# A decoder layer on one core: the weight halves of the front and the queries made once, stored in DRAM and loaded for the second group of tokens

## The chip, the core and the metric

The kernel runs on one core of a Trainium2 chip, as one launch. A core has TensorE (PE: matrix products into PSUM), VectorE (DVE), ScalarE (ACT), GpSimd (POOL), SyncE (SP, which here only issues transfers) and 16 DMA engines that move data between DRAM and on-chip memory. The metric is the device time of the launch in microseconds (us). It was 2892.34 us before the change, the median of three runs from 2890.90 to 2897.49.

## The reference, cut to what matters

One layer over 1024 tokens of width 1024, in fp32:

```
h   = x @ w_in                       # 1024 -> 1792: q 512 | k 128 | v 128 | conv a 512 | conv gate 512
att = window_attention(q, k, v)      # window 128, 8 heads, a sink per head, partial rotary
cnv = swish(LN(causal_conv31(a * sigmoid(gate))))
x1  = LN1(alpha * x + concat(att, cnv) @ w_out)
q   = x1 @ peer_query                # 1024 -> 2048: 8 heads x 2 halves x 128
sc  = q . sub_keys                   # 128 scores per head and half
top 16 of each half, then the 16 best of the 16 x 16 sums -> 128 experts per token, softmax gates
r   = alpha * x1 + sum_e gelu(x1 . u[e]) * gate_e * v[e]    # e among 16384 experts
out = LN2(r + sigmoid(r @ ple_gate) * (p @ ple_proj))
```

The three products with w_in, w_out and peer_query are those that the change touches.

## The kernel before

**Products in three parts.** To keep fp32 accuracy, each operand is split in two: a high half, which is a cast to the rounded format fp32r that PE multiplies, and a low half, which is the operand minus that cast. `mm3` (lines 159 to 162) then issues three matmuls per block of 128: high times high, high times low, low times high. `split` (lines 154 to 157) makes the halves: the cast runs on ACT (it is shown as L156), the subtraction on DVE (L152, in the helper `sub`), and the subtraction needs the cast. For a weight page the two are called `wh<-wraw` and `wl<-wraw,wh`.

**Two groups of tokens.** The 1024 tokens are 8 tiles of 128. Group A is tiles 0 to 2 (384 tokens), group B is tiles 3 to 7 (640 tokens). Each goes through the whole front: w_in, attention, convolution, w_out, LN1, queries. After it the experts of group A are fetched row by row with indirect transfers that POOL issues (`row<-in_peer_u_dram`, `row<-in_peer_v_dram`) and used by DVE (L783 for u, L791 for v), while group B goes through all 16384 experts as dense products (`s_early` for u, and a last stage for v), which fill the rest of the time on PE.

**Weight pages.** A page is 1024 x 128, 512 x 256 or 256 x 512 numbers, 512 KB. `w_split` (lines 270 to 278) makes one: it loads it (`wraw`, issued on SP's queue, L273), and splits it into two more pages `wh` and `wl`. All three come from one pool of six buffers (`wpage`, WPAGES = 6), so two weight pages are in work at a time. Per group there are 14 pages of w_in (8 for the convolution, 2 for k and v, 4 for q), 8 of w_out and 16 of peer_query (one per head and half): 38, and 76 in all, since group B loads and splits the same pages again. `by_token` (L281) multiplies pages for q, k, v and w_out; `by_channel` (L295) those of the convolution and the queries.

**Order.** The work is cut into streams (generators) that yield after each step, and the table `ORDER` and a few calls of `weave` say in which order the steps are written: `c0` and `c1` are the w_in pages of the convolution for group A and B, `t0` and `t1` its 31 taps, done on DVE (`s_taps`, L355 and L357, `cv<-hc,cw,cv`), `q0` and `q1` the pages of q, k and v, `a` attention, `l` the convolution's norm, `w` w_out, `n` LN1, `y` the queries of group A, `h` its choice of experts, `u` the dense products. The queries of group B come in the call `weave((s_query(1), 16), (early, UQ), (rows, RQ))`: 16 steps of queries among dense products and gathered rows. The framework's scheduler then orders each engine's instructions with a timeline that it simulates; only POOL keeps the order written. So the order of DVE, ACT, PE and SP can differ from one version of the kernel to another at places that the source doesn't touch.

**Queries.** `s_query` copies a tile's scores out of PSUM on ACT (L570, `S`, two buffers) and finds the 16 largest per half on DVE (`top16`, L526 to L538: `top<-S`, the replacement `rep` at L534, `top<-rep`).

Of the kernel before, what the change touches and what calls it, by code (L numbers as in the profile page):

```python
# [8 lines left out]
F32 = mybir.dt.float32  # L9
# [10 lines left out]
P = 128  # L20
# [3 lines left out]
KD = D // P  # L24
# [47 lines left out]
def n_split(n):  # L72
    k = -(-n // 512)
    while n % k or (n // k) % 2:
        k += 1
    return [(i * (n // k), n // k) for i in range(k)]
# [22 lines left out]
def layer(tc, io):  # L99
    nc = tc.nc  # L100
    out = io["out"]
    w_in, w_out, w_q = io["w_in"][0], io["w_out"][0], io["peer_query"][0]
    x_d, u_d, v_d = io["x"][0], io["peer_u"][0], io["peer_v"][0]
    groups = [GA, GB]

# [2 lines left out]
    DR = stack.enter_context(tc.tile_pool(name="dram", bufs=1, space=DRAM))  # L108
# [25 lines left out]
    def pt():  # L134
        return PP.tile([P, 512], F32, name="pt")
# [8 lines left out]
    def ph():  # L144
        return PP.tile([P, 512], F32, name="ph", bufs=4)

    def pv():
        return PP.tile([P, 512], F32, name="pv")

    def sub(eng, o, a, b):  # L150

        return eng.tensor_tensor(o, a, b, op=OP.subtract)  # L152

    def split(hi, lo, src, eng):

        nc.scalar.copy(hi, src)  # L156
        return sub(eng, lo, src, hi.bitcast(F32))

    def mm3(ps, lh, ll, rh, rl, first, last):
        nc.tensor.matmul(ps, lh, rh, start=first, stop=False)  # L160
        nc.tensor.matmul(ps, lh, rl, start=False, stop=False)  # L161
        nc.tensor.matmul(ps, ll, rh, start=False, stop=last)  # L162
# [22 lines left out]
    def page(shape, dt, name):  # L185
        return PG.tile(shape, dt, name=name, tag="page", bufs=PAGES)

    def wpage(shape, dt, name):
        return WP.tile(shape, dt, name=name, tag="wpage", bufs=WPAGES)

    def kv(shape, name):
        return WP.tile(shape, F32, name=name, tag="kv", bufs=3)
# [75 lines left out]
                nc.tensor.transpose(ps[:, k * P:(k + 1) * P], src[:, (h + k) * P:(h + k + 1) * P], ident)  # L268
            split(dst[0][:, h:h + 4, sl], dst[1][:, h:h + 4, sl], ps.rearrange("p (k t) -> p k t", k=4), nc.vector)

    def w_split(src, k, n):
        raw = wpage([P, k, n], F32, "wraw")
        nc.sync.dma_start(raw, src.rearrange("(k p) n -> p k n", p=P))  # L273
        hi = wpage([P, k, n], F32R, "wh")
        lo = wpage([P, k, n], F32R, "wl")
        split(hi, lo, raw, nc.vector)
        return hi, lo

    def by_token(gi, src, c0, cn, sink_fn):

        g, (aH, aL) = groups[gi], act[gi]  # L281
        pss = [(ph() if j < 4 else pv())[:, :cn] for j in range(len(g))]
        kn = D // cn
        for kq in range(KD // kn):
            wh, wl = w_split(src[P * kn * kq:P * kn * (kq + 1), c0:c0 + cn], kn, cn)
            for j in range(len(g)):
                sl = slice(j * P, (j + 1) * P)
                for k in range(kn):
                    kk = kn * kq + k
                    mm3(pss[j], aH[:, kk, sl], aL[:, kk, sl], wh[:, k, :], wl[:, k, :], kk == 0, kk == KD - 1)  # L290
                if kk == KD - 1:
                    sink_fn(g[j], pss[j])
            yield

    def by_channel(gi, src, c0, sink_fn):  # L295

        aH, aL = act[gi]
        wh, wl = w_split(src[:, c0:c0 + P], KD, P)
        for (t0, tn) in n_split(len(groups[gi]) * P):
            ps = ph()[:, :tn]  # L300
            for k in range(KD):
                mm3(ps, wh[:, k, :], wl[:, k, :], aH[:, k, t0:t0 + tn], aL[:, k, t0:t0 + tn], k == 0, k == KD - 1)
            sink_fn(ps, t0, tn)
# [8 lines left out]
    def s_qkv(gi):  # L312
        def put_q(i, ps):
            nc.scalar.copy(work[i][:, :512], ps)

        def put_kv(i, ps):
            nc.scalar.copy(
                work[i][:, 512:768].rearrange("p (g u d) -> p g u d", g=2, u=2),
                ps[:, :P].rearrange("p (g d) -> p g d", g=2)[:, :, None, :].to_broadcast([P, 2, 2, 64]))
            vt[i] = work[i][:, 768:896] if i != NA - 1 else W_.tile([P, P], F32, name="vlast")  # L320
            nc.scalar.copy(vt[i], ps[:, P:])

        yield from by_token(gi, w_in, 512, 256, put_kv)
        yield from by_token(gi, w_in, 0, 512, put_q)

    cv, cin = {}, {}

    def s_conv(gi):

        n = len(groups[gi]) * P  # L330
        for bl in range(4):
            sg = W_.tile([P, n], F32, name="sg", bufs=3)
            by_channel(
                gi, w_in, 1280 + P * bl,
                lambda ps, t0, tn: nc.scalar.activation(sg[:, t0:t0 + tn], ps, AF.Sigmoid))
            yield
            hc = cin[gi, bl] = kv([P, HALO + n], "hc")
            nc.vector.tensor_copy(hc[:, :HALO], halo[:, bl, :])
            by_channel(
                gi, w_in, 768 + P * bl,  # L340
                lambda ps, t0, tn: nc.vector.tensor_tensor(hc[:, HALO + t0:HALO + t0 + tn], ps, sg[:, t0:t0 + tn],
                                                           op=OP.mult))
            if gi == 0:
                nc.vector.tensor_copy(halo[:, bl, :], hc[:, n:n + HALO])
            yield
# [138 lines left out]
    def s_wout(gi):  # L484

        for c in range(2):
            cs = slice(512 * c, 512 * c + 512)

            def put(i, ps):
                xc = page([P, 512], F32, "xc")  # L490
                nc.sync.dma_start(xc, x_d[i * P:(i + 1) * P, cs])
                nc.vector.scalar_tensor_tensor(work[i][:, cs], xc, ALPHA, ps, op0=OP.mult, op1=OP.add)
            yield from by_token(gi, w_out, 512 * c, 512, put)

    def layer_norm_stats(pool_, z):
        bs = pool_.tile([P, 2, 6], F32, name="bs", bufs=2)
# [29 lines left out]
    def top16(todo, n):  # L526

        ts = [W_.tile([P, n], F32, name=f"rep{n}", bufs=2 if n == P else 4) for _ in todo]
        for s, v, ix in todo:
            nc.vector.max(v[:, 0:8], s)  # L530
        for s, v, ix in todo:
            nc.vector.max_index(ix[:, 0:8], v[:, 0:8], s)
        for t, (s, v, ix) in zip(ts, todo):
            nc.vector.match_replace(t, v[:, 0:8], s, LOW)  # L534
        for t, (s, v, ix) in zip(ts, todo):
            nc.vector.max(v[:, 8:16], t)
        for t, (s, v, ix) in zip(ts, todo):
            nc.vector.max_index(ix[:, 8:16], v[:, 8:16], t)  # L538
# [3 lines left out]
    def s_query(gi):  # L542

        g = groups[gi]
        n = len(g) * P
        top = W_.tile([P, 2, len(g), 8, 2, 16], U32, name="top", tag=f"cv{gi}")
        for j, i in enumerate(g):
            tv[i], ti[i] = top[:, 0, j].bitcast(F32), top[:, 1, j]
        for h in range(8):
            kr = W_.tile([P, 2, P], F32, name="kr")  # L550
            nc.sync.dma_start(kr, io["peer_keys"][0][h].rearrange("s n c -> n s c"))
            ps = pt()
            for s in range(2):
                nc.tensor.transpose(ps[:, s * P:(s + 1) * P], kr[:, s, :], ident)
            keysT = W_.tile([P, 2, P], F32, name="keysT", bufs=2)
            nc.scalar.copy(keysT, ps[:, :256].rearrange("p (s n) -> p s n", s=2))
            qs = []
            for s in range(2):
                qT = W_.tile([P, n], F32, name="sg", bufs=3)
                by_channel(gi, w_q, 256 * h + P * s, lambda ps, t0, tn: nc.scalar.copy(qT[:, t0:t0 + tn], ps))  # L560
                qs.append(qT)
                if s == 0:
                    yield
            for j, i in enumerate(g):
                ps = pv()
                for s in range(2):
                    nc.tensor.matmul(ps[:, s * P:(s + 1) * P], qs[s][:, j * P:(j + 1) * P], keysT[:, s, :],
                                     start=True, stop=True)
                S = W_.tile([P, 2, P], F32, name="S", bufs=2)
                nc.scalar.copy(S, ps[:, :256].rearrange("p (s n) -> p s n", s=2))  # L570
                top16([(S[:, s, :], tv[i][:, h, s, :], ti[i][:, h, s, :]) for s in range(2)], P)
            yield
# [261 lines left out]
    for v in streams:  # L834
        if v not in "ur":
            assert next(streams[v], 0) == 0, v
    weave((s_query(1), 16), (early, UQ), (rows, RQ))
    weave((s_choose(1), 8 * nB), (early, UC), (rows, RC))
    close(W)
# [95 lines left out]
    n = len(outs) * len(sets)  # L935
    weave((dense, n - RX), (rows, left))
    cn = 256
# [113 lines left out]
```

## Time and profile before

| | |
|---|---|
| device time, median of 3 runs | 2892.34 us (2890.90 to 2897.49) |
| device time of the profiled execution | 2893.7 us |
| its span, first to last instruction | 2891.9 us |
| busy in the span: PE / DVE / ACT / POOL | 2788.4 / 2397.7 / 1195.6 / 1071.4 us |
| moved by the DMA engines | 774.14 MB, mean 268 GB/s |
| loads of weight pages (`wraw`) of w_in / w_out / peer_query | 28 / 16 / 32, 512 KB each |

All durations below come from the profiled execution. Its device time is 1.8 us above its span, for what lies before the first and behind the last instruction, and 1.4 us above the median. The span has 40 slices of 72.3 us on the page. Roughly, by the start times of the weight pages: group A's w_in pages run to 75 us, group B's to 200, attention and w_out of both groups to 430 or so, with the queries of A to 490, the choice of A's experts to 560, and the queries of B to 850. Times are microseconds in every view, except that the ends of matmuls are modelled, so that two in a row overlap in the timeline: how fast they follow each other is read from their starts.

### The profile page before, as it was taken

The page shows a single profiled execution, that of the slowest core. Times are in us where ns is not written, and L with a number is a line of the kernel's source. Part 1 is how long each engine was busy: PE and PEld are TensorE (multiplying, and loading weights), DVE is VectorE, ACT ScalarE, POOL GpSimd, SP SyncE. Part 2 cuts the span into 40 slices and gives each one's busy share as a digit, 9 for nine tenths or more (in the row PEclk, how much of TensorE's full clock was granted, in tenths as well). Part 3 has the DMA queues.
Part 4 walks back from the last instruction along what each step waited for, and adds up shares of the span by engine and source line. Part 5 has one row for each costly group of instructions (what it writes and reads, how often), then busy time and mean ns, then how long its engine had stood idle before and what let it go on. Part 6 is the DMA issues. An engine that isn't in the chain of part 4 may idle for free.

```text
span 2891.9 us, 47040 instructions
## 1 busy us (share of the span) xinstructions
PE 2788.4 (96%) x17619; PEld 2511.6 (87%) x17619; DVE 2397.7 (83%) x5137; ACT 1195.6 (41%) x2468; POOL 1071.4 (37%) x851
## 2 busy tenths in 40 slices
PE   8996899999999999999999999999999999999988
PEld 8974589999989999999999999777777777777788
DVE  7999768979999768777888876888888889888865
ACT  4455644533324466667565742222222222222143
POOL 0103010166671035543444443544444455444420
PEclk9997899999999999999999999999999999999999
DMA  5211343499994359998999898999999999999731
GB/s 157 79 52 41 100 122 108 169 379 323 350 326 169 122 218 373 347 347 332 344 330 357 335 359 312 346 339 344 329 353 345 348 365 339 352 348 337 253 108 46
DMA packets 322836, 774.14 MB, mean 268 GB/s; under 512 B 28945, under 2 KB 144145, under 8 KB 320048
## 3 DMA queue, kind: packets, MB, share of 16 engines
q0 software_dynamic: 110592, 402.70, 38.3%
q1 hardware_dynamic: 212016, 368.44, 36.1%
q8 instruction: 138, 2.26, 0.3%
q14 instruction: 90, 0.74, 0.1%
HBM read 681.78 MB, written 89.26 MB: 267 GB/s over the span
## 4 chain that ended last, share of the span: by engine, by line
PE 87%; DVE 9%; issue 1%; DMA 1%; ACT 1%; SPq 0%; POOL 0%; ACTq 0%; DVEq 0%
PE ph L160 15%; PE ph L161 15%; PE ph L162 15%; PE sum L160 7%; PE sum L161 7%; PE sum L162 6%; PE pv L756 4%; PE pt L661 4%; PE part L160 3%; PE part L162 3%; PE part L161 3%; DVE ag L791 1%; PE pt L674 1%; DVE cv L357 1%; DVE row L783 1%
## 5 line engine op out<-in xcount | busy, mean ns | idle before, releaser
L775 POOL DMA_INDIRECT row<-in_peer_v_dram,ids x384 | 513.1, 1336 | 705.6 <-DVE row L783 538.0
L775 POOL DMA_INDIRECT row<-in_peer_u_dram,ids x384 | 491.7, 1281 | 620.9 <-DVE ag L791 312.4
L160 PE MATMUL ph<-acth,uu 128*128 128x320 f32 x2048 | 651.6, 319 | 0.4 <-ACT uu L663 0.2
L161 PE MATMUL ph<-actl,uu 128*128 128x320 f32 x2048 | 636.7, 311 | 0.2 <-issue 0.2
L162 PE MATMUL ph<-acth,uu 128*128 128x320 f32 x2048 | 635.1, 311 | 0.0
L791 DVE SCALAR_TENSOR_TENSOR ag<-row,hb,ag 128x1024 f32<-128x1024 f32 x384 | 491.4, 1280 | 2.8 <-issue 1.3
L783 DVE SCALAR_TENSOR_TENSOR row<-row,x 128x1024 f32<-128x1024 f32 x384 | 466.8, 1219 | 6.6 <-DMA row<-in_peer_u_dram,ids 6.0
L161 PEld LDWEIGHTS ph<-actl,uu 128*128 128x128 f32 x2048 | 387.1, 189 | 1.2
L160 PEld LDWEIGHTS ph<-acth,uu 128*128 128x128 f32 x2048 | 386.4, 189 | 1.7 <-ACT uu L663 0.5
L162 PEld LDWEIGHTS ph<-acth,uu 128*128 128x128 f32 x2048 | 385.5, 189 | 1.0 <-issue 0.5
L161 PE MATMUL sum<-vl,ah 128*128 128x512 f32 x896 | 350.9, 398 | 0.0
L160 PE MATMUL sum<-vh,ah 128*128 128x512 f32 x896 | 337.0, 399 | 1.3 <-ACT vh L156 0.9
L156 ACT CAST ah<-ge 128x640 fp32r<-128x640 f32 x128 | 92.9, 728 | 562.1 <-DVE ge L870 336.5
L162 PE MATMUL sum<-vh,al 128*128 128x512 f32 x896 | 291.9, 396 | 0.0
L750 ACT ACTIVATE o<-oo,rest 128x128 bf16<-128x128 bf16 x640 | 196.7, 392 | 30.6 <-DVE oo L745 25.9
L160 PEld LDWEIGHTS sum<-vh,ah 128*128 128x128 f32 x896 | 169.6, 189 | 44.3 <-ACT vh L156 1.7
L161 PEld LDWEIGHTS sum<-vl,ah 128*128 128x128 f32 x896 | 169.6, 189 | 41.3
L162 PEld LDWEIGHTS sum<-vh,al 128*128 128x128 f32 x896 | 168.7, 188 | 41.2
L663 ACT CAST uu<-pt 128x512 fp32r<-128x512 f32 x256 | 150.8, 592 | 120.8 <-PE pt L661 111.5
L701 ACT ACTIVATE ge<-ph 128x320 f32<-128x320 f32 x256 | 108.7, 437 | 217.7 <-PE ph L162 183.7
L152 DVE TENSOR_TENSOR vl<-raw,vh 128x1024 fp32r<-128x1024 f32 x128 | 153.9, 1219 | 27.2 <-ACT vh L156 27.1
L160 PE MATMUL part<-vh,ah 128*128 128x512 f32 x384 | 155.0, 404 | 21.8 <-DVE acc L918 13.7
(300 smaller groups left out, 5592.6 us busy)
## 6 DMA issues: line engine op xcount, KB each, us to landing
raw<-in_peer_v_dram SPq DMA_DIRECT2D x128, 512.0 KB
raw<-in_peer_u_dram SPq DMA_DIRECT2D x81, 512.0 KB
g_dr<-stage SPq DMA_DIRECT2D x20, 2048.0 KB
gt<-g_dr SPq DMA_DIRECT2D x21, 1920.0 KB
e_dr<-ge SPq DMA_DIRECT2D x122, 320.0 KB
ge<-e_dr SPq DMA_DIRECT2D x122, 320.0 KB
uraw<-in_peer_u_dram SPq DMA_DIRECT2D x47, 512.0 KB
wraw<-in_peer_query_dram SPq DMA_DIRECT2D x32, 512.0 KB
```

Of the source, the lines that this page charges most:

```text
L152: return eng.tensor_tensor(o, a, b, op=OP.subtract)
L160: nc.tensor.matmul(ps, lh, rh, start=first, stop=False)
L161: nc.tensor.matmul(ps, lh, rl, start=False, stop=False)
L162: nc.tensor.matmul(ps, ll, rh, start=False, stop=last)
L661: nc.tensor.matmul(ps[:, k * P:(k + 1) * P], raws[c][:, (4 * h + k) * P:(4 * h + k + 1) * P], ident, is_transpose=True, start=k == 0, stop ...
L663: nc.scalar.copy(uu[:, 0], turned)
L701: nc.scalar.activation(ge[:, c0:c0 + cn], o, AF.Gelu)
L750: nc.scalar.mul(o2[:, 2, e], oo[:, 1, e], rest[:, t + e:t + e + 1])
L756: nc.tensor.matmul(ps[:, e * P:(e + 1) * P], o2[:, m, 4 * f4 + e], oo[:, 0, 4 * f4 + e], start=m == 0, stop=m == 2)
L775: nc.gpsimd.indirect_dma_start(out=t, out_offset=None, in_=table, in_offset=bass.IndirectOffsetOnAxis(ap=ids[i][:, s:s + 1], axis=0))
L783: behind(nc.vector.scalar_tensor_tensor(u, u, 1.0, x1, op0=OP.mult, op1=OP.mult, accum_out=hb[:, e:e + 1]), marks, TIE)
L791: behind(nc.vector.scalar_tensor_tensor(ag, v, blocks[b][:, e:e + 1], ag, op0=OP.mult, op1=OP.add), marks, TIE)
```

## The change

`w_split` gets the group's number and a key for the page (the weight's name and its place). For group A (`gi == 0`) it loads and splits as before, and then stores both halves in a DRAM tile of their own (`halves`, 2 x 512 KB), two issues on SP's queue. For group B it does neither cast nor subtraction: it loads the two halves into the two pages. `by_token` and `by_channel` take the weight's name in place of its slice; the other edits hand that name on. WPAGES stays at six: in group B three weight pages fit in place of two.

```diff
-    def w_split(src, k, n):
-        raw = wpage([P, k, n], F32, "wraw")
-        nc.sync.dma_start(raw, src.rearrange("(k p) n -> p k n", p=P))
+    halves_dr = {}
+
+    def w_split(gi, key, src, k, n):
+
         hi = wpage([P, k, n], F32R, "wh")
         lo = wpage([P, k, n], F32R, "wl")
-        split(hi, lo, raw, nc.vector)
+        if gi == 0:
+            raw = wpage([P, k, n], F32, "wraw")
+            nc.sync.dma_start(raw, src.rearrange("(k p) n -> p k n", p=P))
+            split(hi, lo, raw, nc.vector)
+            halves_dr[key] = DR.tile([2, P, k, n], F32, name=f"halves{len(halves_dr)}")
+            for j, t in enumerate((hi, lo)):
+                nc.sync.dma_start(halves_dr[key][j], t.bitcast(F32))
+        else:
+            for j, t in enumerate((hi, lo)):
+                nc.sync.dma_start(t.bitcast(F32), halves_dr[key][j])
         return hi, lo
...
-    def by_token(gi, src, c0, cn, sink_fn):
+    def by_token(gi, name, c0, cn, sink_fn):
 
         g, (aH, aL) = groups[gi], act[gi]
+        src = io[name][0]
...
-            wh, wl = w_split(src[P * kn * kq:P * kn * (kq + 1), c0:c0 + cn], kn, cn)
+            wh, wl = w_split(gi, (name, c0, kq), src[P * kn * kq:P * kn * (kq + 1), c0:c0 + cn], kn, cn)
...
-    def by_channel(gi, src, c0, sink_fn):
+    def by_channel(gi, name, c0, sink_fn):
 
         aH, aL = act[gi]
-        wh, wl = w_split(src[:, c0:c0 + P], KD, P)
+        wh, wl = w_split(gi, (name, c0), io[name][0][:, c0:c0 + P], KD, P)
...
-                by_channel(gi, w_q, 256 * h + P * s, lambda ps, t0, tn: nc.scalar.copy(qT[:, t0:t0 + tn], ps))
+                by_channel(gi, "peer_query", 256 * h + P * s, lambda ps, t0, tn: nc.scalar.copy(qT[:, t0:t0 + tn], ps))
```

The lists below give instructions in the order in which an engine takes them: line, operation, output and inputs, shape, and how many alike stand in a row. The first is SP's queue at the start of the program, before the change; `xt` is a tile of x, `wraw` a raw weight page.

```order
L308 DMA xt<-in_x_dram 128x1024 x2
L273 DMA wraw<-in_w_in_dram 128x8x128 x6
L273 DMA wraw<-in_w_in_dram 128x4x256 x2
L273 DMA wraw<-in_w_in_dram 128x2x512 x4
L273 DMA wraw<-in_w_in_dram 128x8x128 x5
```

After the change SP's queue at the same pages reads as follows; `halves` is the DRAM tile of a page, `wh` and `wl` are the stored halves.

```order
L282 DMA halves_325<-wh 128x1024
L278 DMA wraw<-in_w_in_dram 128x8x128
L282 DMA halves_325<-wl 128x1024
L282 DMA halves_362<-wh 128x1024
L278 DMA wraw<-in_w_in_dram 128x8x128
L282 DMA halves_362<-wl 128x1024
L282 DMA halves_399<-wh 128x1024
L278 DMA wraw<-in_w_in_dram 128x8x128
```

Before, loads stood directly behind loads; now each load of a raw page stands between the store of the high half and the store of the low half of the page before it.

On DVE, among group A's first w_in pages, the subtractions (`wl`) and the taps of the convolution (`cv`) alternate; before the change:

```order
L152 TENSOR_TENSOR wl<-wraw,wh 128x1024
L357 SCALAR_TENSOR_TENSOR cv<-hc,cw,cv 128x384 x5
L152 TENSOR_TENSOR wl<-wraw,wh 128x1024
L357 SCALAR_TENSOR_TENSOR cv<-hc,cw,cv 128x384 x5
L152 TENSOR_TENSOR wl<-wraw,wh 128x1024
L357 SCALAR_TENSOR_TENSOR cv<-hc,cw,cv 128x384 x6
L152 TENSOR_TENSOR wl<-wraw,wh 128x1024
```

The same place on DVE after the change:

```order
L151 TENSOR_TENSOR wl<-wraw,wh 128x1024
L367 SCALAR_TENSOR_TENSOR cv<-hc,cw,cv 128x384 x8
L151 TENSOR_TENSOR wl<-wraw,wh 128x1024
L367 SCALAR_TENSOR_TENSOR cv<-hc,cw,cv 128x384 x7
L151 TENSOR_TENSOR wl<-wraw,wh 128x1024
L367 SCALAR_TENSOR_TENSOR cv<-hc,cw,cv 128x384 x8
L151 TENSOR_TENSOR wl<-wraw,wh 128x1024
L367 SCALAR_TENSOR_TENSOR cv<-hc,cw,cv 128x384 x7
```

The scheduler puts 7 or 8 taps between two subtractions, where there were 5 or 6.

On DVE, in the queries of group B, before the change; `ag` and `row` are the uses of gathered rows (v and u), `top` and `rep` belong to the search for the 16 largest scores:

```order
L536 MAX top<-rep_7044 128x8
L152 TENSOR_TENSOR wl<-wraw,wh 128x1024
L536 MAX top<-rep_7045 128x8
L783 SCALAR_TENSOR_TENSOR row,hb<-row,x_6090 128x1024
L538 MAX_INDEX top<-top,rep_7044 128x8
L530 MAX top<-S 128x8 x2
L538 MAX_INDEX top<-top,rep_7045 128x8
L791 SCALAR_TENSOR_TENSOR ag<-row,hb,ag 128x1024
```

And after the change, at the same step of the queries:

```order
L801 SCALAR_TENSOR_TENSOR ag<-row,hb,ag 128x1024
L546 MAX top<-rep_7051 128x8
L546 MAX top<-rep_7052 128x8
L540 MAX top<-S 128x8 x2
L793 SCALAR_TENSOR_TENSOR row,hb<-row,x_6160 128x1024
L548 MAX_INDEX top<-top,rep_7051 128x8
L548 MAX_INDEX top<-top,rep_7052 128x8
L542 MAX_INDEX top<-top,S 128x8 x2
L801 SCALAR_TENSOR_TENSOR ag<-row,hb,ag 128x1024
```

No subtraction of a weight page stands among group B's queries any more. Over the whole program DVE has 38 instructions of that kind fewer and ACT 38 casts; SP has 38 loads of raw pages fewer, and 76 stores and 76 loads of halves more. PE and POOL have the same instructions as before, and PE's order differs only in the front.

## Rows read from the trace of the kernel before

**Rows 1.** The page: busy time and instructions per engine, and PE in 40 slices.

```profile
PE 2788.4 (96%) x17619; PEld 2511.6 (87%) x17619; DVE 2397.7 (83%) x5137; ACT 1195.6 (41%) x2468; POOL 1071.4 (37%) x851
...
PE   8996899999999999999999999999999999999988
```

**Rows 2.** Windows: stretch, length, busy PE, PEld, DVE, ACT, POOL, clock, DMA, GB/s.

```profile
13.00:85.00 72.00, 70.77 (x406) 66.55 (x407) 63.91 (x112) 30.94 (x45) 3.98 (x6) 1.00 0.49 150
85.00:200.00 115.00, 115.00 (x761) 103.76 (x760) 110.46 (x190) 56.02 (x129) 12.51 (x19) 1.00 0.21 63
200.00:300.00 100.00, 74.24 (x355) 50.26 (x354) 96.52 (x147) 52.37 (x129) 23.47 (x28) 0.81 0.15 47
300.00:350.00 50.00, 38.12 (x192) 26.39 (x190) 34.86 (x70) 33.07 (x84) 0.00 (x0) 0.80 0.35 118
430.00:490.00 60.00, 58.28 (x334) 54.95 (x333) 48.29 (x130) 25.04 (x44) 0.00 (x0) 1.00 0.38 110
575.00:625.00 50.00, 50.00 (x348) 49.41 (x347) 42.89 (x88) 18.21 (x38) 35.85 (x27) 1.00 1.03 392
650.00:780.00 130.00, 130.00 (x916) 128.99 (x915) 130.00 (x416) 43.31 (x90) 89.05 (x63) 1.00 0.97 336
780.00:850.00 70.00, 61.82 (x379) 58.36 (x378) 69.17 (x210) 16.86 (x38) 55.15 (x37) 0.88 0.94 323
```

**Rows 3.** The chain of waits, 216 to 275 us: shares by line.

```profile
by line: DVE cv L357 50.0%; DVE sc L400 10.2%; DVE st L406 9.6%; DVE wl L152 7.9%; issue 5.9%; DVE rstd L476 4.3%; DVE cv L478 3.2%; DVE st L408 1.9%; DVE st L409 1.2%; DVE actal L152 1.2%; DVE st L414 1.1%; DVE actl L152 1.0%; DVE cv L355 
```

**Rows 4.** Windows of tile wl alone: stretch, length, DVE busy, clock, DMA, GB/s.

```profile
85.00:200.00 115.00, 17.22 (x15) 1.00 0.21 63
200.00:300.00 100.00, 6.40 (x6) 0.81 0.15 47
560.00:860.00 300.00, 19.52 (x16) 0.97 0.97 345
```

**Rows 5.** Waits (total us, times, longest): DVE 560 to 880, ACT 775 to 860.

```profile
DVE wl L152 <- ACT wh L156: 16.5, 3, 8.1
DVE row L783 <- DMA row<-in_peer_u_dram,ids: 2.5, 3, 1.9
...
ACT S L570 <- DVE rep L534: 20.8, 6, 8.7
```

**Rows 6.** Timeline: start, us, engine, line, operation, tiles, in brackets idle before.

```profile
13.62 1.05 ACT L156 CAST wh<-wraw 128x1024 fp32r<-128x1024 f32 x1 [2.87 <-DMA wraw<-in_w_in_dram]
...
52.52 0.37 SPq L273 DMA_DIRECT2D wraw<-in_w_in_dram  x1
...
56.31 1.05 ACT L156 CAST wh<-wraw 128x1024 fp32r<-128x1024 f32 x1 [3.18 <-DMA wraw<-in_w_in_dram]
...
67.56 2.73 DVE L357 SCALAR_TENSOR_TENSOR cv<-hc,cw,cv 128x384 f32<-128x384 f32 x5
...
74.10 1.05 ACT L156 CAST wh<-wraw 128x1024 fp32r<-128x1024 f32 x1 [3.80 <-DMA wraw<-in_w_in_dram]
...
436.84 1.05 ACT L156 CAST wh<-wraw 128x1024 fp32r<-128x1024 f32 x1 [6.02 <-DMA wraw<-in_peer_query_dram]
...
487.32 1.05 ACT L156 CAST wh<-wraw 128x1024 fp32r<-128x1024 f32 x1 [1.10 <-DVE top L532]
```

**Rows 7.** The chain at the program's start, in order of time: start, us, what.

```profile
7.36 6.24 DMA wraw<-in_w_in_dram
```

**Rows 8.** Timeline of PE: matmuls of 384 columns before and after 22 us.

```profile
20.00 0.52 PE L160 MATMUL ph<-actah,wh 128*128 128x384 f32 x1
20.32 0.52 PE L161 MATMUL ph<-actal,wh 128*128 128x384 f32 x1
...
24.55 0.34 PE L161 MATMUL ph<-actal,wh 128*128 128x384 f32 x1
24.73 0.34 PE L162 MATMUL ph<-actah,wl 128*128 128x384 f32 x1
```

**Rows 9.** Waits of PE, 200 to 350 us: total us, times, longest.

```profile
PE ph L160 <- ACT wh L156: 9.1, 2, 8.6
```

More of the change, by code (lines that the diff above doesn't have):

```diff
@@ L101, in layer @@
     out = io["out"]
-    w_in, w_out, w_q = io["w_in"][0], io["w_out"][0], io["peer_query"][0]
     x_d, u_d, v_d = io["x"][0], io["peer_u"][0], io["peer_v"][0]
@@ L321, in put_kv @@
             nc.scalar.copy(vt[i], ps[:, P:])
-        yield from by_token(gi, w_in, 512, 256, put_kv)
-        yield from by_token(gi, w_in, 0, 512, put_q)
+        yield from by_token(gi, "w_in", 512, 256, put_kv)
+        yield from by_token(gi, "w_in", 0, 512, put_q)
     cv, cin = {}, {}
@@ L333, in s_conv @@
             by_channel(
-                gi, w_in, 1280 + P * bl,
+                gi, "w_in", 1280 + P * bl,
                 lambda ps, t0, tn: nc.scalar.activation(sg[:, t0:t0 + tn], ps, AF.Sigmoid))
@@ L339, in s_conv @@
             by_channel(
-                gi, w_in, 768 + P * bl,
+                gi, "w_in", 768 + P * bl,
                 lambda ps, t0, tn: nc.vector.tensor_tensor(hc[:, HALO + t0:HALO + t0 + tn], ps, sg[:, t0:t0 + tn],
@@ L492, in put @@
                 nc.vector.scalar_tensor_tensor(work[i][:, cs], xc, ALPHA, ps, op0=OP.mult, op1=OP.add)
-            yield from by_token(gi, w_out, 512 * c, 512, put)
+            yield from by_token(gi, "w_out", 512 * c, 512, put)
     def layer_norm_stats(pool_, z):
```

## The prediction, made before the changed kernel ran

> **What bounds the kernel now.** I read the busy times first: TensorE (PE) works in 2788.4 of 2891.9 us [rows 1], so only what it loses elsewhere can be won. The windows show where it loses [rows 2]. From 85 to 200 us, and again from 650 to 780 us, PE is busy all the time at full clock. From 200 to 300 us it is busy 74.24 us at a granted clock of 0.81: at full clock that is 74.24 x 0.81 = 60.1 us of work, so 39.9 us are lost, and VectorE (DVE) is busy 96.5 of these 100 us. From 780 to 850 us PE does 61.82 x 0.88 = 54.4 us of work, 15.6 us lost, with DVE busy 69.2 of 70. The chain of waits for 216 to 275 us says the same by name [rows 3]: half of it is the convolution taps of DVE (cv L357), and wl L152, the low half of a weight page, is 7.9%. So there are two places where DVE makes PE late; everywhere else a lighter DVE is worth nothing at once. After 850 us nothing of the change is left, and a gain at 850 us is carried to the end, since PE is the bound from there on: its row of slices shows a 9 in every one but the last two [rows 1].
>
> **What is removed.** 76 weight pages are made before, 38 for each group of tokens. The second group's 38 pages lose their cast on ScalarE and their subtraction on DVE. On DVE this is 14 pages of w_in (85 to 200 us), 8 of w_out and 16 of the queries (560 to 860 us): by [rows 4] 17.22 us / 15 = 1.15 us each in the first stretch and 19.52 / 16 = 1.22 in the last. That is 14 x 1.15 = 16 us ahead of the first place, 16 x 1.22 = 19.5 us at the second. In the second DVE also stands still for 16.5 us, three times, because the subtraction is next in its queue and the cast has no data yet [rows 5]; that goes too, so DVE is relieved of up to 36 us before 850 us. The 8 subtractions of w_out (near 10 us) lie where PE was the bound and are counted at nothing, and so are the 38 casts (1.05 us each [rows 6]) on ScalarE, which neither of the two places waits for except where it waits for DVE in turn.
>
> **What is added.** In the first group 76 stores of 512 KB, in the second 38 more loads of that size: 114 issues of about 0.37 us on SP's queue [rows 6], 42 us spread over 840, which SP hides, since it waits most of that time. What is not hidden is the order on that queue. Before, the loads of the first group stand behind each other. Now a load stands behind the store of the page before it, and that store waits for the page's cast. So a page's load can only start when the previous page is cast, and cast, issue, load form a loop.
>
> The loop's length: cast 1.05 us, then the store's issue 0.37, then the load. One load, from issue 52.52 to its cast 56.31, takes 3.79 us [rows 6]. How far a store just ahead delays it no row shows. Lower end: not at all, 3.8 us; a gain is excluded, as both use the same 16 engines. Upper end: 6.24 us, the first load of the program, with several tiles of x ahead of it [rows 7]. A store of 0.52 MB at the 392 GB/s of the busiest window [rows 2] would take 1.34 us; I take half of that, 0.7, nearest to the row of the single load, since much of a load's 3.8 us isn't data. With 0.1 us for two hand-overs the loop is 1.05 + 0.37 + 4.5 + 0.1 = 6.0 us, between 5.3 and 7.7.
>
> *First w_in pages.* The first cast is at 13.62 and the fourteenth at 74.10 us [rows 6]: 60.5 / 13 = 4.65 us a page. At 6.0 PE leaves this stage 13 x 1.35 = 17.5 us later. That doesn't reach the end by itself: there are 39.9 us to spare at 200 to 300 us, of which 22 remain. DVE must be counted too. By its new order it does 7 or 8 taps of 0.546 us (five took 2.73 [rows 6]) and one subtraction per page, 7.5 x 0.546 + 1.22 = 5.3 us, so it idles about 0.7 us a page, 9 us, where it idled 8.1 us in 72 before, most of these at the start [rows 2]; I count 6 us more. DVE's net relief ahead of 300 us is 16 - 6 = 10 us, less than PE's 22, so DVE stays the bound there; since both now come out close to each other and wait in turn, I take 8 of the 10. **First place: -8 us**, between +9 (loop of 7.7) and -16 (5.3).
>
> *The first group's w_out pages*: DVE split six in the 100 us from 200 to 300 us [rows 4], 16 us a page, so a loop of 6.0 hides there, and one of 7.7 too.
>
> *The first group's queries.* Six of 16 pages come early, among attention and norms, and are counted at nothing. The other ten go from a cast at 436.84 to one at 487.32 us [rows 6], 50.5 / 9 = 5.6 us apart, with PE busy 58.28 of 60 us [rows 2]. At 6.0 us: 9 x 0.4 = 3.6. **+4 us**, between 0 and +19.
>
> *The second group's queries.* PE can win back at most 15.6 us at 780 to 850 us. What holds it there is DVE: ScalarE waits 20.8 us to copy scores (S L570), until DVE has done with the buffer (rep L534) [rows 5]. A relief of 19.5 to 36 us is enough for all of it, but the transfers grow: 8.4 MB more of loads in some 250 us, beside gathers. Moved were 336 GB/s at 650 to 780 us and 392 at 575 to 625 [rows 2]. The difference, 56 GB/s, is more than the 34 GB/s that come in, so they fit, but nothing is left, and DVE's gather operations, which waited for data only 2.5 us in all [rows 5], will wait more. **-10 us** for the relief, **+2** for gathers; between -15.6 and +25 (8.4 MB at 336 GB/s, nothing of it hidden).
>
> **The sum.** -8 + 4 - 10 + 2 = -12 us. The profiled execution took 2893.7 us, 1.4 above the runs' median of 2892.34, so 2893.7 - 12 is 2881.7; I predict 2881.
>
> **Rivals.**
>
> *Cold clock, slower.* PE would be idle for 1.7 of each 6.0 us in the loop's two stages. At 300 to 350 us it was busy 76% of the time, and the granted clock was 0.80 [rows 2]. At the program's start matmuls of 384 columns followed each other in 0.32 us, later in 0.18 [rows 8]: those are the two levels, 1.2 and 2.4 GHz. A page has 24 of them: 4.3 us warm, 7.7 cold. If the idle stretches bring the clock down, PE itself takes 7.7 us a page: 13 x 3.05 = 40 us late, all the slack; DVE idles 2.4 us a page and 16 us of relief turn into 9 us of loss; the queries lose 9 x 2.1 = 19. 2893.7 + 9 + 19 - 10 + 2 = 2914. It decides as soon as most pages start cold. Against it: each idle stretch is short, while between 200 and 350 us, where the clock fell, a single wait was as long as 8.6 us [rows 9]. The Trainium skill ("TensorE: Matmul & The Clock Gate", section "HAM oscillation — how this bites in real kernels") describes this very pattern, tiles whose compute is shorter than the wait for the next load, each starting cold. There the waits outlast the compute, here they don't; no row settles it.
>
> *The transfers become the bound of the second group's queries, slower.* If 336 GB/s is all that the mix of gathers and loads can do, 8.4 MB cost 25 us and nothing is won: 2893.7 - 8 + 4 + 25 = 2915. For it: the DMA share is 0.97 there; against it the 392 GB/s. The Trainium skill ("DMA: Bandwidth & Descriptors", "Specifications") gives about 358 GB/s of HBM for a core; by it 336 + 34 is too much and some 2 to 3% of the 250 us, an estimated 8 us, would be added instead of 2. The window of 392 GB/s goes beyond that figure, so I keep 2.
>
> *Nothing moves.* PE was full from 650 to 780 us and stays so; the loop eats the first gain: 0 + 4 - 4 + 2, about 2895.
>
> *All hidden.* Stores don't delay loads (loop 5.3), PE's 15.6 us all come back: 2893.7 - 16 - 15.6 = 2862.
>
> That the change doesn't do what it says is excluded by the order: DVE has 38 subtractions fewer.
>
> **How the numbers follow.** Less than 0.2% (5.8 us) can't be told from no change. Chances: forecast 0.50 (2872 to 2892; 0.42 of it faster, 0.08 the same), all hidden 0.13, nothing moves 0.15 (0.12 the same, 0.03 slower), cold clock 0.12, transfers 0.10. Faster 0.55, same 0.20, slower 0.25. The range 2860 to 2908 leaves out the far side of the last two, where they reach their full price, and the best tenth.
>
> **What would show it.** Right: casts of the first 14 pages 6 us apart; no DVE subtraction between 110 and 180 us; DVE still full and PE losing about 30 us at 200 to 300; no ScalarE wait for rep L534 at 780 to 850 and the clock at 1.00 there; DMA at 370 GB/s at 650 to 780. Wrong: a granted clock near 0.5 in the first 110 us, pages 7 us or more apart, DVE waiting tens of microseconds for gathered rows, or PE losing time where it waits for the halves' loads.

## The result, and the profile after

The changed kernel takes 2915.59 us (median of 6 runs, 2910.20 to 2919.21) against 2894.68 for the kernel before (6 runs, 2890.90 to 2897.49). The ratio is 1.0066, 95% interval 1.0056 to 1.0076: it is slower, 21 us, where 2881 was forecast (2860 to 2908). The profiled execution took 2916.42 us (span 2914.5), 22.7 more than the one of before.

The first rows of the page answer to [rows 1]: PE is still busy for 96%, but its first five slices read 7, 8, 9, 8, 7 where 8, 9, 9, 6, 8 stood.

```profile
PE 2799.5 (96%) x17619; PEld 2513.0 (86%) x17619; DVE 2356.8 (81%) x5099; ACT 1157.0 (40%) x2429; POOL 1048.9 (36%) x851
...
PE   7898799999999999999999999999999999999988
```

The windows of the changed kernel, with the stretches and columns of [rows 2]:

```profile
13.00:85.00 72.00, 57.51 (x316) 51.92 (x316) 54.42 (x103) 22.34 (x33) 0.00 (x0) 0.98 0.78 253
85.00:200.00 115.00, 109.51 (x643) 93.71 (x644) 103.77 (x182) 35.90 (x96) 20.97 (x21) 0.97 0.49 171
200.00:300.00 100.00, 85.22 (x473) 64.87 (x471) 84.06 (x129) 58.48 (x141) 24.29 (x32) 0.89 0.37 127
300.00:350.00 50.00, 43.00 (x207) 29.47 (x205) 35.15 (x68) 28.26 (x70) 0.00 (x0) 0.81 0.52 170
430.00:490.00 60.00, 57.35 (x271) 49.96 (x270) 27.24 (x48) 9.51 (x16) 0.00 (x0) 0.97 0.60 207
575.00:625.00 50.00, 50.00 (x347) 49.21 (x346) 47.55 (x221) 20.55 (x39) 25.48 (x21) 1.00 0.77 287
650.00:780.00 130.00, 130.00 (x915) 129.02 (x914) 107.68 (x399) 36.42 (x86) 50.21 (x50) 1.00 0.94 346
780.00:850.00 70.00, 70.00 (x499) 69.40 (x498) 61.42 (x237) 19.91 (x48) 29.77 (x29) 1.00 0.88 317
```

Two rows tell the story. From 780 to 850 us PE is busy for all 70 us at full clock, where [rows 2] had 61.82 at 0.88: this gain came whole. From 13 to 85 us PE is busy for 57.5 us in place of 70.8, and DVE for 54.4 in place of 63.9: both starve together.

Since the two kernels do the same matmuls in nearly the same order, the loss can be placed. I lay the matmuls of a trace in order of start, give each the step to the next that its kind mostly has in the kernel before, and read at which time each kernel has done the same sum. The difference is PE's lag, in us, at the time in the first column (time in the kernel before); e1 to e11 are the experiments below. Each column is one execution: e1 and e9, and the changed kernel and e10, have the same order of instructions up to 2100 us, and still differ by up to 6.4 us in it.

```
 at   after    e1    e2    e3    e4    e5    e6    e7    e8    e9   e10   e11
100    30.3   5.0  30.8  11.3   7.2   3.8   0.0   0.4   0.5   5.3  29.5   7.0
200    30.9   6.0  32.3  12.3   8.2   5.6   0.0   0.4   2.8   6.3  30.1   8.0
240    16.3   2.5  32.7  12.7  12.8   2.5  -0.1   0.7   2.5   1.9  15.5   5.0
340    24.2  -6.2  25.1   8.7  -0.3  -5.0   2.2   5.3  -1.7  -5.5  19.6  -3.7
440    25.0  -5.1  33.2   8.7   0.2  -5.2   8.7   6.2  -1.7  -4.5  21.1  -3.1
560    34.9  -2.1  43.1  15.8   3.2  -5.6  18.5   8.1   0.0  -2.5  28.5   1.1
780    34.0   0.8  44.0  16.9   3.2  -5.6  16.6   7.8   9.5  -4.4  28.0   1.8
860    17.6 -15.7  45.9  17.8 -13.3 -22.1   0.1  -8.7  -6.9 -20.8  11.5 -14.7
2500   17.6 -16.2  39.3  19.4 -13.2 -22.2  -1.0  -8.0  -8.8 -18.2  10.0 -16.3
2880   23.1  -4.2  49.4  25.5  -6.5 -14.9   4.9   7.3  -1.6 -18.3   9.7 -16.6
```

The changed kernel is 30 us late after the first group's w_in pages, gets 14 of them back by 240 us and loses 8 again by 340, loses 10 in the first group's queries, wins 16.4 at 780 to 860, and loses 5.5 in the last stage: 30.3 - 14 + 8 + 10 - 16.4 + 5.5 = 23.

How the 30 us come about stands in the timeline. These are SP's issues and ACT's casts in the changed kernel, 44 to 60 us (start, us, engine, line, operation, tiles, in brackets the idle time before):

```profile
44.94 1.05 ACT L155 CAST wh<-wraw 128x1024 fp32r<-128x1024 f32 x1 [2.65 <-DVE cv L367]
51.59 1.04 ACT L155 CAST wh<-wraw 128x1024 fp32r<-128x1024 f32 x1 [4.19 <-DVE cv L367]
58.27 1.04 ACT L155 CAST wh<-wraw 128x1024 fp32r<-128x1024 f32 x1 [5.25 <-DVE cv L367]
...
46.01 0.32 SPq L282 DMA_DIRECT2D halves<-wh  x1
46.42 0.39 SPq L278 DMA_DIRECT2D wraw<-in_w_in_dram  x1
47.27 0.61 SPq L282 DMA_DIRECT2D halves<-wl  x1
```

The store of the high half is issued at 46.01, as the cast ends (44.94 + 1.05); the next load follows at 46.42, and its cast starts at 51.59. A page is 1.05 + 0.43 + 5.17 = 6.65 us. The releaser in the brackets (DVE cv) is not the one that held the cast: the taps had been done before, and the load's last landing event is at 51.48. SP's waits from 25 to 105 us, before and after (waiting line, releaser, total us, times, longest), say who holds the queue:

```profile
SPq L273 <- PE ph L162: 69.3, 15, 6.6
```

```profile
SPq L282 <- ACT wh L155: 60.5, 12, 6.9
```

Before, SP waited until PE had finished with a page buffer, to load the next page into it. Now it waits for the cast, at the head of the store, with the load behind it.

### The profile page after: what moved, and what is told of

It is laid out like the page before. It is cut to its first block, busy times and chain, and to the rows that moved or that the text cites. A ratio compares the mean times of both kernels' runs of the same rounds, so it can differ in the third digit from the quotient of the medians.

```text
span 2914.5 us, 47161 instructions
## 1 busy us (share of the span) xinstructions
PE 2799.5 (96%) x17619; PEld 2513.0 (86%) x17619; DVE 2356.8 (81%) x5099; ACT 1157.0 (40%) x2429; POOL 1048.9 (36%) x851
## 5 line engine op out<-in xcount | busy, mean ns | idle before, releaser
L785 POOL DMA_INDIRECT row<-in_peer_v_dram,ids x384 | 498.9, 1299 | 682.7 <-DVE row L793 469.9
L785 POOL DMA_INDIRECT row<-in_peer_u_dram,ids x384 | 477.5, 1244 | 669.6 <-DVE ag L801 313.5
L161 PE MATMUL sum<-vh,al 128*128 128x512 f32 x896 | 285.4, 396 | 0.0
```

What stands on the lines that cost most here:

```text
L785: nc.gpsimd.indirect_dma_start(out=t, out_offset=None, in_=table, in_offset=bass.IndirectOffsetOnAxis(ap=ids[i][:, s:s + 1], axis=0))
```

## The experiments

Each ratio is against runs of the kernel before on the same chip.

**Theories.** "Order": the loss is the load's place behind a store that waits for the cast. "Bytes": the stores take the DMA engines, wherever they stand. Later came a third, "order of the last stage": the scheduler writes the end of the program anew.

**e1: stores behind the next load.** The two stores of a page are held back until the next page's load is issued, and tied behind it:

```diff
+            load = nc.sync.dma_start(raw, src.rearrange("(k p) n -> p k n", p=P))
+            store_halves(load)
...
+                st = nc.sync.dma_start(dr[j], t.bitcast(F32))
+                if load is not None:
+                    tc.add_manual_dep(st.ins, load.ins.name,
```

> All halves as in the changed kernel, but on SP's queue the two stores of a page are put behind the load of the next raw page. In the changed kernel a page of the first stage took 6.66 us, cast to cast: 1.05 cast, 0.43 to the load's issue behind the store, 5.1 load; before, 4.65 with a load of 3.8. Theory 'order' (the load stands behind a store that waits for the cast): the load is issued early again, pages come in 4.7 to 5.0 us, TensorE's work is late by under 6 us at 100 us instead of 30, and the time falls to 2875 to 2890. Theory 'bytes' (the stores take the DMA engines, so a load takes 5.1 us wherever it stands): pages of 6.0 us, 18 us late at 100 us, time 2900 to 2910.

2887.86 us, ratio 0.997 (0.9958 to 0.9983): faster than before, and 28 us faster than the changed kernel by an order alone. The lag is 5 us at 100 us. "Order" holds. Part of "bytes" holds too: the fourteen casts run from 13.46 to 80.00 us, 5.1 us a page, and a load issued at 51.10 has its cast only at 57.09, 6 us later; but it is issued before the cast (53.42) of the page ahead of it, and well before that page's store (54.49):

```profile
51.10 0.56 SPq L286 DMA_DIRECT2D wraw<-in_w_in_dram  x1
54.49 0.32 SPq L276 DMA_DIRECT2D halves<-wh  x1
```

```profile
53.42 1.05 ACT L155 CAST wh<-wraw 128x1024 fp32r<-128x1024 f32 x1 [4.17 <-DMA wraw<-in_w_in_dram]
57.09 1.05 ACT L155 CAST wh<-wraw 128x1024 fp32r<-128x1024 f32 x1 [1.25 <-DMA wraw<-in_w_in_dram]
```

**e2: stores alone.** `if gi == 0` governs the store only; the second group splits as before.

> The first group stores all halves as in the changed kernel, the second group loads raw pages and splits them as before; nothing reads the stored halves. This is the cost side alone. If the whole loss is made by the stores and their place in the queue, TensorE's work is 30 us late at 100 us as in the changed kernel, the 17 us it wins back at 780 to 860 us are missing, and the relief ahead of 300 us too: 2893 + 23 + 17 to 30 = 2933 to 2946. If the loads of halves were part of the loss, or the scheduler's other order, the time would be near the changed kernel's 2916 or lower.

2946.0 us, ratio 1.0181 (1.0168 to 1.0194), the upper end of what was expected. The lag is 30.8 at 100 us, as in the changed kernel, and the win at 780 to 860 us is gone. So the loss needs no load of halves; e2 also loses 10 us in the last stage.

**e3: small stores alone.** As e2, with

```diff
-                    nc.sync.dma_start(halves_dr[key][j], t.bitcast(F32))
+                    nc.sync.dma_start(halves_dr[key][j][:8], t.bitcast(F32)[:8])
```

> As the run with stores alone, but each store moves only 8 of the 128 partitions, 1/16 of the bytes, from the same place in SP's queue with the same wait for the cast; nothing reads them. 'Order': the load still starts about 1.5 us after the cast's start and takes 3.8 us, pages in 5.3 us, 8 us late at 100 us (with the first pages' delay up to 12). 'Bytes': pages in 4.7 us, nothing late. Time by 'order' 2893 to 2905, by 'bytes' 2893. The difference to the run with full stores is the share of the bytes: 1.3 us a page by the rows, 17 us at 100 us.

2918.39 us, ratio 1.0084 (1.0071 to 1.0097). The pages and the lag at 100 us came as "order" said:

```profile
48.30 1.05 ACT L155 CAST wh<-wraw 128x1024 fp32r<-128x1024 f32 x1 [3.45 <-DMA wraw<-in_w_in_dram]
53.76 1.05 ACT L155 CAST wh<-wraw 128x1024 fp32r<-128x1024 f32 x1 [3.92 <-DMA wraw<-in_w_in_dram]
```

```profile
49.38 0.26 SPq L283 DMA_DIRECT2D halves<-wh  x1
49.69 0.40 SPq L278 DMA_DIRECT2D wraw<-in_w_in_dram  x1
```

5.46 us a page with a load of 4.07 from issue to cast, and 11.3 us late at 100 us. So at 100 us the queue alone costs 11 us, the bytes alone (e1) 5, and both together 31: beside a full store a load takes 5.2 us in place of 4.1, and only behind the store does the load's length count in full. But the time was missed by 13 us: the 11 us were not caught up at 200 to 300, the first group's queries added 7, and the last stage took 8.

**e4: stores issued by GpSimd.** `nc.gpsimd.dma_start` for the two stores.

> All halves as in the changed kernel, but the stores are issued by GpSimd, so that SP's queue holds loads alone in the order of before. 'Order': pages in 4.7 to 5.0 us, time 2875 to 2890, as with the stores behind the next load. 'Bytes': pages in 6.0 us and 2900 to 2910. A third way: the six page buffers are held until the stores have read them (3.1 us behind the cast for the high half, 5.5 for the low), so the load is late although no store stands ahead of it; then pages stay near 6 us here and with stores behind the next load alike, while small stores alone are fast.

2887.05 us, ratio 0.9976 (0.9967 to 0.9986): the same as e1 by another way of freeing the load. The third way, that the stores hold the page buffers, falls. The Trainium skill (Trainium Kernel Development and Optimization, "Key Constraints") says that issuing DMAs from several engines saves only the sequencer's issue time. This run differs: an issue of a store takes 0.32 to 0.61 us, 0.9 us a page, while a page of the first stage took 5.3 us (casts from 13.26 to 81.97 us) where the changed kernel's took 7.0 (13.64 to 105.09). What goes besides the issue time is the wait at the head of the queue.

**e5: loads alone.** The halves of three pages are stored, and the second group loads those in place of its own 38.

> The second group loads halves as in the changed kernel, but the first group stores them only for three pages, one of each shape, and the second group reads these three again and again (its weights are the wrong ones, so its part of the output isn't the reference's; the work per page is the same). The gain side alone. If the relief is worth what the changed kernel's trace against the stores alone suggests, TensorE's work is 16 us ahead at 240 us, the first group's pages stay at 4.7 us, and another 16 us come at 780 to 860: 2895 - 16 to - 33 = 2862 to 2879. If the relief ahead of 300 us is spent again by 340 us (there the changed kernel and the stores alone stand within 1 us of each other), it is 2877 to 2880. If loads of halves cost as much as the splits, 2890 or more.

2878.5 us, ratio 0.9944 (0.9928 to 0.9959), the second of the three cases. The lag at 340 us is -5.0, and 16.5 more come at 780 to 860. That is what the change can win almost without its stores, in this order of instructions: the three pages still cost 3.8 us at 100 us, and the last stage gives back 7.3.

**e6 and e7: queries alone**, in the changed order and with the stores behind the load.

> Only the 16 pages of peer_query are stored and loaded again, in the changed kernel's order (a load behind the store of the page before); w_in and w_out are split twice as before. If the parts add up as read from the lags of the two traces (first group's queries 10 us lost, second group's 16.5 won, some 6 lost in the last 400 us): 2895 - 6.5 + 0 to 6 = 2888 to 2895. If the loss in the front is what makes the win at 780 to 860 us possible, the win is missing and the time is 2900 or more.

> As the run with the queries alone, but each page's stores stand behind the load of the next raw page. By 'order' the first group's queries lose 0 to 4 us instead of 10, so 2878 to 2886, some 7 us faster than with the changed order. By 'bytes' both are alike.

2903.66 us, ratio 1.0028 (1.0018 to 1.0038), and 2901.11, ratio 1.002 (1.001 to 1.003): both missed. The win at 780 to 860 us is there in both, 16.5 us. In e6 the lag grew by 16 us between 340 and 560, in the first group's queries, and not by 10. In e7 they lose 3 us, within the 0 to 4 that "order" gave; the rest of its miss lies elsewhere. PE is 4.6 us late at 280 us, before its first query page is loaded at 303, although up to 300 us every engine takes the instructions in the same order as in the kernel before. All but 0.4 us of it comes between 254 and 263 us, and the granted clock tells it: windows of PE, PEld, DVE, ACT, POOL, clock, DMA and GB/s, before and then e7.

```profile
250.00:256.00 6.00, 4.10 (x22) 2.90 (x18) 6.00 (x10) 4.25 (x9) 5.84 (x8) 0.74 0.01 3
256.00:262.00 6.00, 4.93 (x33) 3.31 (x32) 6.00 (x9) 1.17 (x2) 2.50 (x5) 0.98 0.00 0
```

```profile
250.00:256.00 6.00, 3.94 (x25) 2.73 (x25) 6.00 (x10) 4.15 (x9) 5.84 (x8) 0.82 0.01 3
256.00:262.00 6.00, 5.33 (x21) 3.42 (x21) 6.00 (x8) 1.28 (x3) 2.96 (x5) 0.50 0.00 0
```

The clock is at 0.50, the lower of its two levels, where it was 0.98, after PE had been busy 3.94 of 6 us (4.10 before). So these 4 us are not the change's: one execution can lose them to the clock with the order unchanged. And 15 us go between 2500 and 2880. These two runs led to the theory on the last stage.

**e8: only the low half stored**, behind the load; the second group loads raw page and low half and casts again.

> All three weights; only the low half is stored, behind the next raw load, and the second group loads the raw page and the low half and casts the high half again on ScalarE (1.05 us each, 38 casts more than in the changed kernel). Half the stored bytes. With both halves stored behind the load the first group's w_in pages came 5.1 us apart and TensorE's work was 6 us late at 200 us. If that rest is the bytes, pages come at 4.8 to 4.9 us, 3 us late, and the time is 2882 to 2886 (2888 with both halves). If it is the wait of the six buffers for the stores, it stays at 6 us and 2888. If the casts on ScalarE cost as the splits did, the win at 780 to 860 us is gone: 2900.

2890.37 us, ratio 0.9974 (0.9965 to 0.9983). With half the bytes stored the first stage was as hoped (0.5 us late at 100 us): what e1 still lost there was the bytes. But PE lost 9.5 us between 560 and 780 us (e1: 2.9), where the second group's casts are back on ScalarE. PE's waits from 560 to 800 us are on ScalarE, for the casts of pages (wh) and for other tiles that stand in its queue with them, 7.3 us in all:

```profile
PE pt L700 <- ACT uu L689: 3.0, 5, 1.2
PE pt L687 <- ACT keysT L582: 2.2, 1, 2.2
PE ph L159 <- ACT wh L301: 2.1, 2, 1.6
```

**e9 and e10: the last stage's order held.** Every instruction of PE, DVE, ACT and SP from the first load of the v table on is chained to the one that stands before it in the kernel before:

```diff
+    for engine in ('PE', 'DVE', 'Activation', 'SP'):
...
+                tc.add_manual_dep(seen[f"I-{at}"], f"I-{last}",
+                                  mybir.DependencyInfo(mybir.DependencyClass.NoSync, mybir.DependencyReason.DATA),
+                                  reason="order of the last stage")
```

> All halves, stores behind the next raw load, and in the last stage (from the first load of the v table on) the instructions of TensorE, VectorE, ScalarE and SyncE are held in the order that they have in the kernel before. Without that order held, the kernel was 15.7 us ahead of before at 860 us and only 4.2 ahead at the end: 11.5 us were lost between 2400 and 2800 us. Theory 'order of the last stage' (the scheduler, given another front, writes the last stage in another order, in which TensorE waits more for VectorE's sums): the 15.7 us stay, the time falls from 2888 to 2877 to 2880. Rival: the loss is phase (gathered rows and transfers arrive elsewhere in time, since everything is 16 us earlier): the time stays at 2886 to 2890.

> The changed kernel with nothing else altered than the last stage's order, held as before. It was 17.6 us late at 860 us and 23.1 at the end. 'Order of the last stage': 2910 (5 to 6 us faster than the changed kernel). 'Phase': 2914 to 2916.

2872.84 us, ratio 0.9917 (0.9904 to 0.993), and 2905.14, ratio 1.0034 (1.0022 to 1.0046): e1 and the changed kernel gained 15 and 10 us, more than expected. In the table the lag of both stays within 0.3 us from 2500 to 2880, where the unheld ones lose 5.5 and 12. Windows of PE, PEld, DVE, ACT, POOL, clock, DMA and GB/s for 2560 to 2720 us show it: the kernel before, the changed one, e1, e9 and e10, in this order.

```profile
2560.00:2720.00 160.00, 158.44 (x676) 126.80 (x675) 139.75 (x173) 38.45 (x47) 74.67 (x57) 1.00 0.92 326
```

```profile
2560.00:2720.00 160.00, 153.82 (x648) 121.05 (x648) 133.15 (x168) 38.72 (x47) 67.99 (x54) 1.00 0.96 338
```

```profile
2560.00:2720.00 160.00, 154.50 (x648) 122.41 (x647) 129.43 (x158) 35.54 (x44) 71.81 (x53) 0.99 0.88 307
```

```profile
2560.00:2720.00 160.00, 159.22 (x679) 127.79 (x679) 135.15 (x168) 34.91 (x43) 70.25 (x54) 1.00 0.88 316
```

```profile
2560.00:2720.00 160.00, 158.44 (x676) 126.88 (x675) 136.84 (x172) 38.14 (x47) 72.06 (x56) 1.00 0.92 330
```

PE is busy for 158.4 us or more with the order of before and for 153.8 and 154.5 without. From 2350 us on PE waits 7.3 us for DVE's sums (`part<-acc`) in the kernel before, e9 and e10, but 12.2 in the changed kernel and 9.7 in e1. The rival (phase) falls: e9 is 18 us early there and loses nothing. Up to the last stage e9 and e1 have the same order, and so have e10 and the changed kernel; yet the profiled executions differ by 5 to 6 us at 860 us. That is how much one execution can differ from another there. It may be why e9 and e10 gained more than the 12 and 5.5 us of the last stage; no run shows it.

**e11: w_in and queries alone**, behind the load, last stage held.

> Halves stored for w_in and peer_query alone, behind the next raw load, w_out split twice as before; the last stage held as before. If the 8 stored pages of w_out cost the first group more than the 8 subtractions saved, the time is 2 to 8 us under the run with all three weights and the last stage held (2877 to 2880 by 'order of the last stage'), so 2870 to 2877; if w_out's pages were hidden both ways, the same as that run.

2876.82 us, ratio 0.9933 (0.992 to 0.9947). Not faster than e9: its interval (0.992 to 0.9947) and e9's (0.9904 to 0.993) overlap, so storing w_out is no loss that these runs show. e9 is the best version: by the ratios 24 us faster than before and 43 faster than the change.

## Why the prediction was wrong, step by step

**The loop of cast, store and load** was the right mechanism, and its size was off. Forecast were 6.0 us a page (5.3 to 7.7); the pages from the third to the fourteenth took 6.66 (casts at 31.85 and 105.09, 73.24 / 11), and the first two gaps, among the tiles of x, 10.3 and 7.9. PE came out 30 us late, not 17.5. The load beside a store took 5.2 us, not 4.5. That alone doesn't explain the miss: even pages of 7.7 us were priced at +9 us for the first place, and at 6.66 PE is 24 us late at 340.

**"39.9 us to spare at 200 to 300 us"** is the step that failed. I counted PE's idle time there as room that a late PE could use, because DVE was the bound, and let DVE lose only 6 us of its own. That fails in two ways. First, DVE's subtractions stand in its queue between the taps and wait for the same casts. DVE's windows from 13 to 110 us, of the kernel before, the changed kernel, e3 and e1 (length, busy, clock, DMA, GB/s):

```profile
13.00:110.00 97.00, 88.92 (x155) 1.00 0.43 131
```

```profile
13.00:110.00 97.00, 74.07 (x138) 0.95 0.77 248
```

```profile
13.00:110.00 97.00, 78.50 (x137) 1.00 0.44 130
```

```profile
13.00:110.00 97.00, 89.48 (x163) 0.96 0.87 303
```

DVE idles 8.1 us before, 22.9 in the changed kernel, 18.5 in e3 and 7.5 in e1. Its wait for the casts in this stretch, before and after:

```profile
DVE wl L152 <- ACT wh L156: 3.0, 6, 0.7
```

```profile
DVE wl L151 <- ACT wh L155: 18.7, 13, 4.8
```

Second, what DVE does at 200 to 300 us is fed by PE. These are all engines from 200 to 250 us (columns of [rows 2]), and the last gate products of the second group's convolution on DVE, before and after:

```profile
200.00:250.00 50.00, 36.92 (x175) 25.56 (x175) 48.19 (x68) 26.00 (x56) 15.12 (x17) 0.86 0.20 63
```

```profile
200.00:250.00 50.00, 50.00 (x311) 40.27 (x310) 38.65 (x55) 25.94 (x56) 2.35 (x4) 1.00 0.30 103
```

```profile
213.35 0.88 DVE L341 TENSOR_TENSOR hc<-ph,sg 128x320 f32<-128x320 f32 x2
```

```profile
248.32 0.48 DVE L351 TENSOR_TENSOR hc<-ph,sg 128x320 f32<-128x320 f32 x1
```

PE, late with the second group's pages, is now full there, and DVE, which was full, idles 11.4 of 50 us. A full DVE at 200 to 300 us, which the prediction named as a sign of being right, did not come: it is busy for 84.06 of 100. DVE's windows from 13 to 340 us, before and after, add it up:

```profile
13.00:340.00 327.00, 301.22 (x505) 0.91 0.28 87
```

```profile
13.00:340.00 327.00, 269.46 (x456) 0.93 0.52 175
```

DVE is busy 31.8 us less. 17.4 of these are the 14 subtractions that are gone (`wl` alone: 46.83 us before, 29.43 after); the other 14.4 us are work that it had done by 340 us before the change and has still to do now. So DVE idles 31.8 us more by 340 us, 14.8 of them up to 110 us and 9.5 between 200 and 250: the whole relief, and 14.4 us besides. How much of PE's 24 us comes by each of the two ways, no run separates.

e3 shows the consequence without any relief of DVE: 11.3 us late at 100 us, 12.3 at 200 and 8.7 at 340, 3.6 us recovered of 39.9 "to spare". Where the first group's pages are hardly delayed, the relief does arrive: from 100 to 340 us e1 wins 11.2 us and e5 8.8, near the 8 that were forecast. In the changed kernel it shows only for a while: at 240 us it stands at 16.3 and e2, which differs by the second group's splits, at 32.7; by 340 us the two stand at 24.2 and 25.1. Why the changed kernel loses 8 us again from 240 to 340 (e10, with the same order there, loses 4), in a stretch in which the scheduler has written the first group's w_out and attention in another order, is open.

**The first group's w_out pages**, said to hide, belong to that open stretch. **The first group's queries** cost 10 us, not 4, inside the range of 0 to 19.

**The second group's queries** were right in mechanism, and too small in size: 10 us of relief less 2 for gathers were forecast. At 780 to 850 us PE had 15.6 us to win back, and every kernel that loads the halves of the queries won 16.4 or 16.5, whether it came 34 us late or 5.6 early. The wait for rep went from 20.8 us [rows 5] to 6.5 and reached PE no more; DVE waited more for gathered rows, as said, and that cost nothing, since PE was full. ACT's wait at 775 to 860 us, then DVE's at 560 to 880:

```profile
ACT S L580 <- DVE rep L544: 6.5, 4, 2.1
```

```profile
DVE row L793 <- DMA row<-in_peer_u_dram,ids: 8.9, 9, 2.2
DVE ag L801 <- DMA row<-in_peer_v_dram,ids: 6.9, 7, 1.4
```

**"A gain at 850 us is carried to the end"** was wrong too, by 5.5 us: the lag is 17.6 us at 860 and at 2500 us, but the scheduler writes the last stage anew. PE's order differs there too, from 2358 us on in the trace of the kernel before; that it differs only in the front, as said with the change, was a misreading.

**The rivals.** The clock did not go cold: 0.98 in the first stage, with PE idle for 14.5 us of 72. The transfers did not become a bound: 346 GB/s and a full PE at 650 to 780 us. "Nothing moves" had the loop eat the first gain, which is nearer to what happened, but saw no loss in it. My slower cases asked for a cold PE or a full DMA; the real one needed only that the loop's delay reaches DVE as well, by the casts and by PE's late products.

## What to carry to other kernels

A store that waits for an engine delays everything behind it on its queue: tie it behind the next load, or issue it elsewhere; here that is worth 28 us of 2916. Idle time of an engine at a later place is room for a delay only if whatever holds it there is neither held by the same delay nor fed by the late engine. And where a scheduler orders the program as a whole, compare stages that the change doesn't touch too, and hold their order before judging an edit.

## What was not expected of the hardware

A store of 1/16 of the bytes does not land in 1/16 of the time. In e3 a store of 8 partitions of 4 KB had its last landing event 1.8 us after the issue for the high half (49.38 to 51.15) and 2.9 for the low one (50.63 to 53.56); the full 128 partitions took 3.1 (52.66 to 55.78) and 5.5 (47.27 to 52.73) in the changed kernel. And loads and stores of 512 KB side by side kept the DMA engines busy for 0.97 of the time from 13 to 85 us in e9, at 334 GB/s, while a page still came every 5.1 us (casts from 13.67 to 80.02).
